# A hybrid decoder layer: another order for squares, roots, products and gates in the Z stage

## The chip, the core and the metric

The kernel runs on one core of one Trainium2 chip. Its five engines each work through an instruction queue of their own, in order: TensorE (PE, matmuls), VectorE (DVE), ScalarE (ACT), GpSimd (POOL) and SyncE (SP, which issues most DMAs). An instruction waits on semaphores that instructions of other engines, or DMAs, raise. The metric is the device time of one execution in microseconds; for one core this is the time of that core.

## The reference

One layer with two groups of heads on 1024 tokens of 1024 features, in float32. Cut to its frame:

```python
h = rms_norm(x, norm1_w[l])
proj = h @ w_in[l]
da_q, da_k, da_v, dn_qkv, dn_z, dn_a, dn_b = jnp.split(
    proj, [SPLIT_1, SPLIT_2, SPLIT_3, SPLIT_4, SPLIT_5, SPLIT_6], axis=-1)
...
dn_o = rms_norm(dn_o, dn_out_norm_w[l]) * jax.nn.silu(dn_z.reshape(B, S, DN_HEADS, DN_V_DIM))
...
x = x + mix @ w_out[l]
h = rms_norm(x, norm2_w[l])
x = x + jnp.square(jax.nn.relu(h @ w_up[l])) @ w_down[l]
```

The change is in the part that makes, for every token, the normed input `h`, the gate `silu(dn_z)` (512 columns, multiplied with `dn_out_norm_w`) and the 8 columns `dn_a`, `dn_b`. The rest (differential attention, the gated delta rule, output projection, MLP) is not touched.

## The kernel before

**Stages.** The Z stage comes first: it norms x, keeps the result for all later stages and makes the gate. Then follow the dn projections with the chunk matrices of the delta rule, the scan interleaved with attention, the output projection, and the MLP. Float32 products are made of three matmuls in the type fp32r: each operand is split into a rounded high part (`hH`, `wH`) and the rest (`hL`, `wL`), and high x high, high x low and low x high are added (L311 to L313).

**Row blocks.** The 1024 tokens are 8 blocks of 128 (`tb` 0 to 7). A block of x is loaded twice: transposed (`xTs[tb]`, features on partitions) and as rows (`xts[tb]`). The norm of a block takes these steps:

- `z_square` (L358): ACT squares the rows and adds them up per token (L361).
- `z_root` (L364): DVE forms mean plus epsilon (`nrt`, L223), POOL raises it to the power -1/2 (`nr`, L224).
- `z_diag` (L369): ACT scales an identity matrix with the roots (`dg`, L372).
- `z_spread` (L374): PE multiplies a matrix of ones with that diagonal (`ps_r`, L377). Every partition then holds the roots of the 128 tokens. It is issued inside a product, ahead of the product's step k = `at` (2 where nothing else is given).
- `z_scale` (L380 to L396): DVE multiplies the 8 feature blocks of `xT` with norm weight and roots (L388; L385 for blocks 0 and 1, which are weighed beforehand), ACT rounds two halves into `hH` (L389), DVE subtracts two halves into `hL` (L392).

**Products.** The 520 columns of gate, a and b are two units of 260 (`u` 0, 1). For blocks 0 and 1 the products run on the unscaled x (`z_raw`, L316, plain float32), and their roots are multiplied in afterwards; for blocks 2 to 7 `z_mm` (L303) makes 24 matmuls of 260 columns on `hH` and `hL`. Blocks 0 and 1 are scaled too, as later stages need them. The results lie in PSUM banks of three pools with two banks each: `pj`, `ph` and `pt_`. A fourth pool, `pm`, holds the spreads. In the kernel before, blocks 0 and 1 use `pj` (unit 0) and `ph` (unit 1), block 2 uses `pt_`, and blocks 3 to 7 only `pj`.

**Gates.** `z_gate` (L325) reads a product: a tanh on ACT (`zth`, L330), then on DVE (tanh + 1) times the product (`zg`, L331). For blocks 0 and 1 (`raw`) a second DVE instruction multiplies with root and norm weight (L334), and L338 takes the 8 columns of a and b; for the others POOL multiplies with the weight (L336) and L340 takes the 8 columns. SP stores the gate (L341). A bank comes free with its last reader: L331 for unit 0, L338 or L340 for unit 1. The gate's weight `dnw4` is halved and copied on POOL (L452, L453).

**Order.** In the Z stage the order on PE, DVE, ACT and POOL is the order in which the code is written (`tc.manual_schedule`); an instruction that waits holds up all that stand behind it on its engine. Ahead of the changed part, blocks 2 and 3 are scaled and the raw products made. In the loop over blocks 3 to 7, block tb's two products are written, then block tb+2 is scaled (its spread is in the second product), then block tb+3 is squared, rooted and made a diagonal, with the two gates of block tb among them.

**What comes behind.** `load_unit` (L183) loads 256-column units of the dn weights in four parts (`wraw`, two buffers), rounds each on ACT (L192) and subtracts on DVE (L193). The first unit takes the weight tiles of z unit 0, so its rounding can begin only when z(7,0) is done. From a and b of all blocks follow beta (L539 to L541) and the decays (L547 to L567); from those come the matrices `rrh` and `rrl` (L666) and products on PE (L668). POOL clears some tiles there (L587, L726). `trn` (L198 to L200) makes the dn products. Outside the Z stage a scheduler orders the instructions; apart from a few places next to the stage its order is the same in both kernels.

Of the kernel before, what the change touches and what calls it, by code (L numbers as in the profile page):

```python
# [22 lines left out]
NT = SEQ // P  # L23
# [97 lines left out]
def tile_hymba_layer(  # L121
# [99 lines left out]
    def rstd(o, ss, scale, eps, pool, tag, n):  # L221
        t = pool.tile([P, n], F32, tag=tag, name=tag) if pool else laid(tag)
        V.tensor_scalar(t, ss, scale, eps, ALU.mult, ALU.add)  # L223
        G.tensor_tensor(o, t, neghalf[:, :n], ALU.pow)  # L224
# [15 lines left out]
    pj = pctx.enter_context(tc.tile_pool(name="pj", bufs=2, space=PSUM))  # L240
    p1ctx = ctx.enter_context(ExitStack())
    ph = p1ctx.enter_context(tc.tile_pool(name="ph", bufs=2, space=PSUM, side="right"))
    pm = p1ctx.enter_context(tc.tile_pool(name="pm", bufs=2, space=PSUM, side="right"))
    pt_ = p1ctx.enter_context(tc.tile_pool(name="pt_", bufs=2, space=PSUM, side="right"))
# [58 lines left out]
    def z_mm(tb, u, pool=pj, tag="pj", mid=None, at=2):  # L303

        ps = pool.tile([P, 512], F32, tag=tag, name="ps_z")
        sl = slice(tb * P, (tb + 1) * P)
        wh, wl = wz[u][0]
        for k in range(KB):
            if k == at and mid is not None:
                z_spread(mid)  # L310
            T.matmul(ps[:, :UC], hH[:, k, sl], wh[:, k, :], start=k == 0, stop=False)  # L311
            T.matmul(ps[:, :UC], hH[:, k, sl], wl[:, k, :], start=False, stop=False)
            T.matmul(ps[:, :UC], hL[:, k, sl], wh[:, k, :], start=False, stop=k == KB - 1)  # L313
        return ps

    def z_raw(tb, u, pool, tag, mid=None, at=2):  # L316

        ps = pool.tile([P, 512], F32, tag=tag, name="ps_z")
        for k in range(KB):
            if k == at and mid is not None:  # L320
                z_spread(mid)
            T.matmul(ps[:, :UC], xTs[tb][:, k, :], wz[u][1][k // 2][:, k % 2, :], start=k == 0, stop=k == KB - 1)
        return ps

    def z_gate(tb, u, ps, raw=False):  # L325
        n = UC if u == 0 else 252
        th = n1.tile([P, UC], F32, tag="zth", name="zth", bufs=2)
        zg = n1.tile([P, UC], F32, tag="zg", name="zg", bufs=7)
        r = roots[tb]
        S.activation(th[:, :n], ps[:, :n], AF.Tanh, scale=half_r[tb] if raw else 0.5)  # L330
        last = V.scalar_tensor_tensor(zg[:, :n], th[:, :n], 1.0, ps[:, :n], ALU.add, ALU.mult)  # L331
        w = dnw4[:, UC * u:UC * u + n]
        if raw:
            last = V.scalar_tensor_tensor(zg[:, :n], zg[:, :n], r, w, ALU.mult, ALU.mult)  # L334
        else:
            G.tensor_tensor(zg[:, :n], zg[:, :n], w, ALU.mult)  # L336
        if u == 1 and raw:
            last = V.tensor_scalar(ab[:, tb, :], ps[:, 252:260], r, None, ALU.mult)  # L338
        elif u == 1:
            last = V.tensor_copy(ab[:, tb, :], ps[:, 252:260])  # L340
        nc.sync.dma_start(zg_d[tb, :, UC * u:UC * u + n], zg[:, :n])  # L341
        return last

    def z_round(u, i):
        S.copy(wz[u][0][0][:, 2 * i:2 * i + 2], wz[u][1][i])

    def z_rest(u, i):
        wh, wl = [x[:, 2 * i:2 * i + 2] for x in wz[u][0]]
        V.tensor_tensor(wl, wz[u][1][i], wh.bitcast(F32), ALU.subtract)
# [3 lines left out]
    def z_weigh(tb):  # L353
        for c in cuts:
            V.tensor_tensor(xTs[tb][:, c, :], xTs[tb][:, c, :], w1c[:, c].unsqueeze(2).broadcast_to([P, 4, P]),
                            ALU.mult)

    def z_square(tb):  # L358
        sq = n1.tile([P, DM], F32, tag="sq", name="sq", bufs=1)
        ss = n1.tile([P, 1], F32, tag="nss", name="nss", bufs=4)  # L360
        S.activation(sq, xts[tb], AF.Square, accum_out=ss)  # L361
        sums[tb] = ss

    def z_root(tb):  # L364

        r = roots[tb] = n1.tile([P, 1], F32, name=f"nr{tb}")
        rstd(r, sums[tb], 1.0 / DM, EPS, n1, "nrt", 1)

    def z_diag(tb):  # L369

        diags[tb] = n1.tile([P, P], F32, tag="dg", name="dg", bufs=4)
        S.activation(diags[tb], ident, AF.Copy, scale=roots[tb])  # L372

    def z_spread(tb):  # L374

        ps = pm.tile([P, 512], F32, tag="pm", name="ps_r")
        marks[tb] = T.matmul(ps[:, :P], ones, diags[tb], start=True, stop=True)  # L377
        spreads[tb] = ps[:, :P]

    def z_scale_parts(tb):  # L380
        sl = slice(tb * P, (tb + 1) * P)
        xT, last = xTs[tb], []
        for c in cuts:
            if tb < 2:
                V.tensor_tensor(xT[:, c, :], xT[:, c, :], spreads[tb].unsqueeze(1).broadcast_to([P, 4, P]), ALU.mult)  # L385
            else:
                for k in range(c.start, c.stop):
                    V.scalar_tensor_tensor(xT[:, k, :], xT[:, k, :], w1c[:, k:k + 1], spreads[tb], ALU.mult, ALU.mult)  # L388
            last.append(S.copy(hH[:, c, sl], xT[:, c, :]))  # L389
        yield  # L390
        for c in cuts:
            last.append(V.tensor_tensor(hL[:, c, sl], xT[:, c, :], hH[:, c, sl].bitcast(F32), ALU.subtract))  # L392
        yield last

    def z_scale(tb):
        return list(z_scale_parts(tb))[1]  # L396
# [17 lines left out]
    marks = {}  # L414
    with tc.manual_schedule(engines={T.engine, V.engine, S.engine, G.engine}):

        pw = pm.tile([P, 512], F32, tag="pm", name="ps_w")
        for i in range(10):
            T.transpose(pw[:, 0:P], ident, ident)
        z_weigh(0)  # L420
        z = {(0, 0): z_raw(0, 0, pj, "pj")}
        for i in range(3):
            z_round(0, i)
            z_rest(0, i)
        z_weigh(1)
        z_round(0, 3)
        z_rest(0, 3)
        z[1, 0] = z_raw(1, 0, pj, "pj")
        for i in range(4):
            z_round(1, i)  # L430
            z_rest(1, i)
        z_square(2)
        z_root(2)
        z_diag(2)
        z[0, 1] = z_raw(0, 1, ph, "ph", 2, 6)
        z_square(3)
        z_root(3)
        z_diag(3)
        z[1, 1] = z_raw(1, 1, ph, "ph", 3, 4)
        z_scale(2)  # L440
        z_square(0)
        z_square(1)
        parts = z_scale_parts(3)
        next(parts)
        for tb in range(2):
            z_root(tb)
        next(parts)
        for tb in range(2):
            half_r[tb] = n1.tile([P, 1], F32, name=f"hr{tb}")
            V.tensor_scalar(half_r[tb], roots[tb], 0.5, None, ALU.mult)  # L450
        z_square(4)
        G.tensor_scalar(dnw4[:, 0], dnw4[:, 0], 0.5, None, ALU.mult)  # L452
        G.tensor_copy(dnw4[:, 1:4], dnw4[:, 0:1].broadcast_to([P, 3, P]))  # L453
        dnw4 = dnw4.rearrange("p h e -> p (h e)")
        z[2, 0] = z_mm(2, 0, pt_, "pt")
        z_gate(0, 0, z[0, 0], True)
        z_root(4)
        z_diag(4)
        z_gate(1, 0, z[1, 0], True)
        z_gate(0, 1, z[0, 1], True)  # L460
        z[2, 1] = z_mm(2, 1, pt_, "pt", 4, 6)
        z_scale(4)
        z_square(5)
        z_gate(2, 0, z[2, 0])
        z_root(5)
        z_diag(5)
        z_gate(1, 1, z[1, 1], True)
        z_gate(2, 1, z[2, 1])
        for tb in range(3, NT):
            late = tb - 4 if 4 <= tb < 6 else None  # L470
            z[tb, 0] = z_mm(tb, 0, mid=late)
            if late is not None:
                z_scale(late)
            z[tb, 1] = z_mm(tb, 1, mid=tb + 2 if tb + 2 < NT else None)
            z_gate(tb, 0, z[tb, 0])
            if tb + 2 < NT:
                last = z_scale(tb + 2)
                if tb == 3:
                    mark = [marks[5], *last]
            if tb + 3 < NT:  # L480
                z_square(tb + 3)
                z_root(tb + 3)
                z_diag(tb + 3)
            if 3 <= tb < 5:
                z_diag(tb - 3)
            z_gate(tb, 1, z[tb, 1])


    behind = ExitStack()
# [56 lines left out]
    u, au, e, w1, lw, d1, z1 = (n32(n) for n in ("gu", "gau", "gte", "gw1", "glw", "gd1", "gz1"))  # L546
# [272 lines left out]
    pools, T_ops = {}, []  # L819
# [127 lines left out]
    late, accs = [], {}  # L947
# [393 lines left out]
    normed_by, normed_at, held_back, banks, normed2, raws, kept, u, ups = [], {}, [], {}, set(), [], {}, {}, {}  # L1341
# [410 lines left out]
    last = u_raw(4)  # L1752
# [76 lines left out]
```

## Time and profile before

| | us |
|---|---|
| median of 3 runs | 1265.45 |
| lowest, highest | 1264.93, 1265.61 |
| the profiled execution | 1262.67 |
| its span (first to last instruction) | 1261.0 |
| its mean granted PE clock | 0.996 of full speed |

A row of the view in order of time has the start in us, the duration in us, engine, line, operation, the tile written and the tiles read with their shapes, the count, and in brackets the engine's idle time before it with what ended it. A row of a stage has its limits and length, then for PE, PEld (weight load), DVE, ACT and POOL the busy us with the number of instructions, then the mean granted PE clock, the share of the DMA engines that is busy, and GB/s. The chain of waits is followed back from the last instruction to whatever released each step.

### The profile page before, as it was taken

Reading aid. Unit: us, or ns where it says so; the run is one execution under the profiler, and the core shown is the slowest. Engines: PE = TensorE matmul, PEld = TensorE weight load, DVE = VectorE, ACT = ScalarE, POOL = GpSimd, SP = SyncE. Lnnn points to the kernel's source line nnn. Section 1 sums busy time; section 2 is a strip of 40 time slices with the busy share of each in tenths; the row PEclk is TensorE's granted clock in tenths of the full one; section 3 lists DMA queues with packets and bytes.
Section 4 is the critical chain, followed back from the end, with each engine's and each line's share of the span. In section 5 each row is a group of like instructions: output and inputs, shape, how many; then the busy total and the mean of one; then the engine's idle time right before and its main releaser. Section 6 shows DMA issues by size and latency. Waiting matters only on the chain.

```text
span 1261.0 us, 18863 instructions
## 1 busy us (share of the span) xinstructions
PE 1229.8 (98%) x6887; PEld 1058.9 (84%) x6887; DVE 826.1 (66%) x1466; ACT 617.4 (49%) x1243; POOL 107.7 (9%) x139
## 2 busy tenths in 40 slices
PE   8799999999999999999999999999999999999998
PEld 7688888899998897888888888888888888888887
DVE  5757798657647647767599656655569855677553
ACT  5459654334336545666567445544555333333331
POOL 1221110012213210001210000000000000000000
PEclk9899999999999999999999999999999999999999
DMA  9134554356858656423254545343469655422311
GB/s 338 65 93 123 131 169 124 91 180 213 269 156 236 190 170 170 116 73 95 87 184 152 205 161 184 134 167 127 174 234 341 259 200 200 167 100 100 130 38 67
DMA packets 157637, 202.11 MB, mean 160 GB/s; under 512 B 20921, under 2 KB 110825, under 8 KB 157545
## 3 DMA queue, kind: packets, MB, share of 16 engines
q1 hardware_dynamic: 157400, 200.91, 49.1%
q8 instruction: 54, 0.88, 0.3%
q14 instruction: 39, 0.31, 0.1%
q10 hardware_dynamic: 144, 0.00, 0.0%
HBM read 135.86 MB, written 65.01 MB: 159 GB/s over the span
## 4 chain that ended last, share of the span: by engine, by line
PE 89%; DMA 4%; DVE 3%; ACT 2%; issue 1%; SPq 1%; POOL 0%; DVEq 0%; ACTq 0%; POOLq 0%
PE X L1428 5%; PE X L1429 5%; PE X L1430 5%; PE X L1728 4%; PE X L1727 4%; PE X L1726 4%; PE ps_dn L198 3%; PE ps_dn L200 3%; PE ps_dn L199 3%; PE ps_qk L992 3%; PE ps_qk L994 3%; PE ps_qk L993 3%; PE Y L1428 2%; PE Y L1429 2%; PE Y L1430 2%; PE ps_op L1257 2%
## 5 line engine op out<-in xcount | busy, mean ns | idle before, releaser
L1346 ACT CAST hH<-ur 128x1024 fp32r<-128x1024 f32 x56 | 58.8, 1051 | 173.3 <-PE Y L1727 90.1
L1347 DVE TENSOR_TENSOR hL<-ur,hH 128x1024 fp32r<-128x1024 f32 x56 | 68.4, 1223 | 80.3 <-ACT hH L1346 80.3
L992 PE MATMUL ps_qk<-wH,hH 128*128 128x256 f32 x384 | 114.9, 299 | 0.1
L994 PE MATMUL ps_qk<-wH,hL 128*128 128x256 f32 x384 | 108.5, 282 | 0.0
L993 PE MATMUL ps_qk<-wL,hH 128*128 128x256 f32 x384 | 108.4, 282 | 0.0
L1347 DVE TENSOR_TENSOR op<-raw,op 128x1024 fp32r<-128x1024 f32 x48 | 58.7, 1223 | 73.8 <-PE X L1429 40.8
L1726 PE MATMUL X<-hH 128*128 128x512 f32 x224 | 87.1, 389 | 0.0
L1727 PE MATMUL X<-hL,hH 128*128 128x512 f32 x224 | 87.1, 389 | 0.0
L1728 PE MATMUL X<-hH,hL 128*128 128x512 f32 x224 | 87.1, 389 | 0.0
L198 PE MATMUL ps_dn<-hH,wH 128*128 128x512 f32 x192 | 76.2, 397 | 0.2 <-ACT cp L611 0.2
L200 PE MATMUL ps_dn<-hH,wL 128*128 128x512 f32 x192 | 76.0, 396 | 0.0
L199 PE MATMUL ps_dn<-hL,wH 128*128 128x512 f32 x192 | 75.8, 395 | 0.0
L992 PEld LDWEIGHTS ps_qk<-wH,hH 128*128 128x128 f32 x384 | 73.5, 191 | 0.3 <-ACT qn L1011 0.2
L993 PEld LDWEIGHTS ps_qk<-wL,hH 128*128 128x128 f32 x384 | 73.5, 191 | 0.0
L994 PEld LDWEIGHTS ps_qk<-wH,hL 128*128 128x128 f32 x384 | 73.2, 191 | 0.0
L1347 DVE TENSOR_TENSOR hL<-dw,hH 128x1024 fp32r<-128x1024 f32 x56 | 68.1, 1218 | 0.9 <-ACT hH L1346 0.9
L1346 ACT CAST op<-raw 128x1024 fp32r<-128x1024 f32 x48 | 50.4, 1051 | 36.0 <-PE Y L1430 19.9
L193 DVE TENSOR_TENSOR wL<-wraw,wH 128x512 fp32r<-128x512 f32 x64 | 43.7, 696 | 34.8 <-ACT wH L192 34.5
L1346 ACT CAST hH<-dw 128x1024 fp32r<-128x1024 f32 x56 | 58.7, 1049 | 10.7 <-DMA dw<-in_w_down_dram 5.0
L192 ACT CAST wH<-wraw 128x512 fp32r<-128x512 f32 x64 | 38.2, 620 | 45.2 <-DMA wraw<-in_w_units_dram 31.7
L615 DVE SCALAR_TENSOR_TENSOR cy<-cp,pv,cy 128x512 f32<-128x512 f32 x72 | 53.7, 747 | 8.1 <-ACT cy L613 7.3
L1121 ACT ACTIVATE pexp<-ps_sc,mx 128x128 f32<-128x128 f32 (+7 forms) x64 | 47.3, 740 | 20.0 <-DVE mx L1117 19.9
(362 smaller groups left out, 3442.0 us busy)
## 6 DMA issues: line engine op xcount, KB each, us to landing
ur<-ud SPq DMA_DIRECT2D x28, 1024.0 KB, 5.1
raw<-in_w_up_dram SPq DMA_DIRECT2D x32, 512.0 KB, 4.0
dw<-in_w_down_dram SPq DMA_DIRECT2D x32, 512.0 KB, 6.5
wraw<-in_w_units_dram SPq DMA_DIRECT2D x48, 256.0 KB, 3.7
qk_d<-qa SPq DMA_DIRECT2D x32, 256.0 KB, 3.4
ud<-ua SPq DMA_DIRECT2D x16, 512.0 KB, 4.1
ud<-s SPq DMA_DIRECT2D x16, 512.0 KB, 2.6
pka<-park_d SPq DMA_DIRECT2D x32, 192.0 KB, 4.2
```

The lines of the kernel that those rows point to most:

```text
L198: T.matmul(ps, lh(k), rh(k), start=(k == 0), stop=False)
L199: T.matmul(ps, lh(k), rl(k), start=False, stop=False)
L200: T.matmul(ps, ll(k), rh(k), start=False, stop=(k == n - 1))
L992: T.matmul(ps[:, :256], hH[:, k, sl], wh[:, k, :], start=(k == 0), stop=False)
L993: T.matmul(ps[:, :256], hH[:, k, sl], wl[:, k, :], start=False, stop=False)
L994: T.matmul(ps[:, :256], hL[:, k, sl], wh[:, k, :], start=False, stop=(k == KB - 1))
L1346: S.copy(dst[0], src)
L1347: V.tensor_tensor(dst[1], src, dst[0].bitcast(F32), ALU.subtract)
L1428: T.matmul(ps, op[0][:, k, cs], h[0][:, k, :], start=start and k == 0, stop=False, skip_group_check=True)
L1726: T.matmul(bank[t], v[0][:, j, sl], v[2][:, j], start=s0, stop=False, skip_group_check=True)
L1727: T.matmul(bank[t], v[0][:, j, sl], v[3][:, j], start=False, stop=False, skip_group_check=True)
L1728: T.matmul(bank[t], v[1][:, j, sl], v[2][:, j], start=False, stop=s1, skip_group_check=True)
```

## The change

Only the manual order of the Z stage changes, and the banks that its products use:

- Root and diagonal of block 4 come right behind its square, ahead of the first gate; block 5 is squared between the first two gates, block 6 ahead of z(3,0), block 7 ahead of z(3,1).
- Blocks 3 to 7 use the pools `pj`, `ph`, `pt_`, `pj`, `ph` in turn, six banks instead of two.
- The spreads move: block 4's into z(3,0) at step 1, 5's into z(3,1) at step 3, 6's into z(4,1) at 1, 7's into z(5,0) at 3, 0's into z(5,1) at 3, 1's into z(6,0) at 3. The scaling of each follows the product that holds its spread.
- The gates are written by a list behind these scalings: those of (0,1) and (1,1) behind z(3,0), of block 2 behind z(3,1), of block 3 behind z(4,1), of block 4 behind z(5,0), and so on; the last two behind z(7,1).
- The diagonals of blocks 0 and 1 both come behind that of block 7.

In the order that results outside the Z stage three things differ: the transposition to `ps_pv`, which uses a bank of `ph`, stands in the first dn product instead of between z(3,1) and z(4,0); DVE has L540 and L541 ahead of the L193 of the third weight part instead of behind it; and on SP the stores of the gates stand elsewhere among the small loads. Lines behind the changed part are two higher in the kernel after.

```diff
         z_square(4)
+        z_root(4)
+        z_diag(4)
         G.tensor_scalar(dnw4[:, 0], dnw4[:, 0], 0.5, None, ALU.mult)
         G.tensor_copy(dnw4[:, 1:4], dnw4[:, 0:1].broadcast_to([P, 3, P]))
         dnw4 = dnw4.rearrange("p h e -> p (h e)")
+
+        pools = {3: (pj, "pj"), 4: (ph, "ph"), 5: (pt_, "pt"), 6: (pj, "pj"), 7: (ph, "ph")}
         z[2, 0] = z_mm(2, 0, pt_, "pt")
         z_gate(0, 0, z[0, 0], True)
-        z_root(4)
-        z_diag(4)
+        z_square(5)
+        z[2, 1] = z_mm(2, 1, pt_, "pt")
         z_gate(1, 0, z[1, 0], True)
-        z_gate(0, 1, z[0, 1], True)
-        z[2, 1] = z_mm(2, 1, pt_, "pt", 4, 6)
-        z_scale(4)
-        z_square(5)
-        z_gate(2, 0, z[2, 0])
+        roots_due = {(3, 0): (6,), (3, 1): (7,)}
+        gates_due = {(3, 0): ((0, 1), (1, 1)), (3, 1): ((2, 0), (2, 1)), (4, 1): ((3, 0), (3, 1)),
+                     (5, 0): ((4, 0), (4, 1)), (5, 1): ((5, 0),), (6, 0): ((5, 1),), (6, 1): ((6, 0),),
+                     (7, 0): ((6, 1),), (7, 1): ((7, 0), (7, 1))}
+        spread_at = {(3, 0): (4, 1), (3, 1): (5, 3), (4, 1): (6, 1), (5, 0): (7, 3), (5, 1): (0, 3), (6, 0): (1, 3)}
         z_root(5)
         z_diag(5)
-        z_gate(1, 1, z[1, 1], True)
-        z_gate(2, 1, z[2, 1])
         for tb in range(3, NT):
-            late = tb - 4 if 4 <= tb < 6 else None
-            z[tb, 0] = z_mm(tb, 0, mid=late)
-            if late is not None:
-                z_scale(late)
-            z[tb, 1] = z_mm(tb, 1, mid=tb + 2 if tb + 2 < NT else None)
-            z_gate(tb, 0, z[tb, 0])
-            if tb + 2 < NT:
-                last = z_scale(tb + 2)
-                if tb == 3:
-                    mark = [marks[5], *last]
-            if tb + 3 < NT:
-                z_square(tb + 3)
-                z_root(tb + 3)
-                z_diag(tb + 3)
-            if 3 <= tb < 5:
-                z_diag(tb - 3)
-            z_gate(tb, 1, z[tb, 1])
+            for u in range(2):
+                for b in roots_due.get((tb, u), ()):
+                    z_square(b)
+                nxt, at = spread_at.get((tb, u), (None, 0))
+                z[tb, u] = z_mm(tb, u, *pools[tb], nxt, at)
+                if nxt is not None:
+                    last = z_scale(nxt)
+                    if nxt == 5:
+                        mark = [marks[5], *last]
+                for b in roots_due.get((tb, u), ()):
+                    z_root(b)
+                    z_diag(b)
+                if (tb, u) == (3, 1):
+                    z_diag(0)
+                    z_diag(1)
+                for b, v in gates_due.get((tb, u), ()):
+                    z_gate(b, v, z[b, v], b < 2)
```

## The prediction

> **What bounds the kernel now.** First the page: span, busy shares, chain.
>
> ```profile
> span 1261.0 us, 18863 instructions
> ...
> PE 1229.8 (98%) x6887; PEld 1058.9 (84%) x6887; DVE 826.1 (66%) x1466; ACT 617.4 (49%) x1243; POOL 107.7 (9%) x139
> ...
> PE 89%; DMA 4%; DVE 3%; ACT 2%; issue 1%; SPq 1%; POOL 0%; DVEq 0%; ACTq 0%; POOLq 0%
> ```
>
> TensorE (PE) is 98% busy, so only a stage with PE gaps can give anything. Next the busy time by stage: the Z products that the change reorders (21.4 to 74.8), the start of the dn projections, what follows.
>
> ```profile
> 21.40:74.80 53.40, 42.05 (x303) 40.97 (x302) 34.71 (x105) 23.30 (x51) 13.29 (x19) 0.90 0.32 113
> 74.80:89.00 14.20, 12.77 (x61) 10.11 (x59) 8.54 (x28) 8.24 (x20) 3.59 (x7) 1.00 0.50 130
> 89.00:200.00 111.00, 111.00 (x597) 93.29 (x598) 92.03 (x237) 77.53 (x255) 16.14 (x15) 1.00 0.52 142
> ```
>
> In the Z stage PE is idle for 11.4 us and its clock averages 0.90; after 89 us it is busy without a gap for over 100 us. So an earlier Z end moves everything behind it by as much. Third, PE in order of time:
>
> ```profile
> 24.50 0.28 PE L311 MATMUL ps_z<-wH,hH 128*128 128x260 f32 x1
> ...
> 26.52 0.28 PE L313 MATMUL ps_z<-wH,hL 128*128 128x260 f32 x1
> 28.98 0.76 PE L377 MATMUL ps_r<-dg,ones 128*128 128x128 f32 x2 [2.17 <-ACT dg L372]
> ...
> 30.19 0.42 PE L311 MATMUL ps_z<-wH,hH 128*128 128x260 f32 x1
> ...
> 32.14 0.42 PE L311 MATMUL ps_z<-wH,hH 128*128 128x260 f32 x1
> ...
> 37.63 0.49 PE L377 MATMUL ps_r<-dg,ones 128*128 128x128 f32 x2 [2.31 <-ACT dg L372]
> ...
> 45.54 0.49 PE L377 MATMUL ps_r<-dg,ones 128*128 128x128 f32 x2 [4.17 <-ACT dg L372]
> ...
> 56.23 0.70 PE L377 MATMUL ps_r<-dg,ones 128*128 128x128 f32 x2 [2.70 <-ACT dg L372]
> ...
> 74.80 0.40 PE L198 MATMUL ps_dn<-hH,wH 128*128 128x512 f32 x1
> ```
>
> Four stalls, 11.35 us, all at a spread (L377) that waits for its diagonal (L372), the end of square, root, diagonal. The 0.28 us rows are 17 steps apart, 0.119 us each; the 0.42 us rows 9 steps, 0.217 us: after the gaps of 2.17, 4.17 and 2.70 the first 15 or so matmuls run at half speed (1.5 us lost each), after that of 2.31 they do not. A product is 24 steps, 2.87 us.
>
> **The change part by part.** No arithmetic is added: 12 products, 6 spreads, the same gates. What changes is the order on each engine, so I walk it, writing z(b,u) for block b, unit u. Prices come from rows where the consumer was waiting (ACT, then DVE, then POOL):
>
> ```profile
> 14.24 1.06 ACT L361 ACTIVATE sq<-xt 128x1024 f32<-128x1024 f32 x1 [1.93 <-DMA xt<-in_x_dram]
> ...
> 16.25 0.40 ACT L372 ACTIVATE dg<-ident,nr 128x128 f32<-128x128 f32 x1 [0.86 <-POOL nr L224]
> ...
> 25.19 1.06 ACT L361 ACTIVATE sq<-xt 128x1024 f32<-128x1024 f32 x1 [0.70 <-DMA xt<-in_x_dram]
> ...
> 32.31 0.62 ACT L389 CAST hH<-xT 128x512 fp32r<-128x512 f32 x1 [2.66 <-DVE xT L388]
> 33.35 0.63 ACT L389 CAST hH<-xT 128x512 fp32r<-128x512 f32 x1 [0.41 <-DVE xT L388]
> ...
> 37.17 0.40 ACT L372 ACTIVATE dg<-ident,nr 128x128 f32<-128x128 f32 x1 [1.88 <-POOL nr L224]
> 37.48 0.45 ACT L330 ACTIVATE zth<-ps_z,hr 128x252 f32<-128x252 f32 x1
> ```
>
> ```profile
> 15.43 0.15 DVE L223 TENSOR_SCALAR nrt<-nss 128x1 f32<-128x1 f32 x1 [2.06 <-ACT sq L361]
> ...
> 31.16 2.15 DVE L388 SCALAR_TENSOR_TENSOR xT<-xT,w1c,ps_r 128x128 f32<-128x128 f32 x8
> 33.23 1.47 DVE L392 TENSOR_TENSOR hL<-xT,hH 128x512 fp32r<-128x512 f32 x2
> ...
> 37.96 0.42 DVE L331 SCALAR_TENSOR_TENSOR zg<-zth,ps_z 128x252 f32<-128x252 f32 x1 [2.15 <-ACT zth L330]
> 38.41 0.48 DVE L334 SCALAR_TENSOR_TENSOR zg<-zg,nr,dnw 128x252 f32<-128x252 f32 x1
> 38.81 0.22 DVE L338 TENSOR_SCALAR ab<-ps_z,nr 128x8 f32<-128x8 f32 x1
> 38.95 0.41 DVE L331 SCALAR_TENSOR_TENSOR zg<-zth,ps_z 128x252 f32<-128x252 f32 x1
> ```
>
> ```profile
> 15.66 0.55 POOL L224 TENSOR_TENSOR nr<-nrt,neghalf 128x1 f32<-128x1 f32 x1 [13.17 <-DVE nrt L223]
> ...
> 25.69 0.62 POOL L452 TENSOR_SCALAR dnw<-dnw 128x128 f32<-128x128 f32 x1
> 26.38 0.50 POOL L453 COPY dnw<-dnw 128x384 f32<-128x384 f32 x1
> ```
>
> Root chain: square to nrt 1.19, nrt to nr 0.23, nr to diagonal 0.59; 0.31 later ACT issues the next. Raw gate: tanh to L331 0.48, to L334 0.45, to L338 0.40, next gate 0.14 on. Scaling: casts 1.15 and 2.19 after the first L388, the low part done at 3.54.
>
> *Block 4.* Its square stays at 25.19, but root and diagonal now come before the gate of z(0,0): diagonal at 25.19+1.19+0.23+0.59=27.20, and the first stall is gone. That gate's tanh, which came right behind the square, moves behind the diagonal to 27.51. z(3,0) reuses its bank and now waits for L331 to end, 28.42, while PE has finished z(2,1) at 24.50+2.87=27.37: a new stall of 1.1. The weights of the gate (L452, L453) stand behind nr4 on POOL: 25.19+1.19+0.23=26.61, +0.55+1.19=28.35, in time for L334 at 28.45.
>
> *Blocks 5 and 6.* Square 5 at 27.88, tanh of z(1,0) 28.94, L331 29.43, L334 29.88, and only then nrt5 at 30.29: diagonal 31.11, in time for its spread at 32.8. The scaling of block 4 starts at 30.37. Square 6 takes ACT from 31.42 to 32.48, so the cast due at 31.52 waits 1.0; second low part from 33.73, nrt6 34.34, diagonal 6 at 35.16. Square 6 needs its row block, which is issued here and lands at 29.7 by the DMA row; were it 1 us later, all below is 0.4 late.
>
> ```profile
> 22.22 1.41 SPq L277 DMA_DIRECT2D xt<-in_x_dram  x2
> ...
> DMA to landing us min/median/max: 7.5/7.5/7.5
> ```
>
> *The third bank pair.* z(4,0) takes the bank of z(0,1), whose gate stands behind diagonal 6 on ACT: tanh 35.47, L331 35.96, L334 36.41, L338 36.81, bank free 37.05. PE is through with z(3,1) at 28.45+0.2 (the first matmul after a wait)+2x(2.87+0.24)=34.9, a spread being two matmuls or 0.24. Second new stall, 2.2. Behind that diagonal also wait tanh(1,1), square 7 and the casts of block 5.
>
> *Block 7.* Gate of z(1,1) on DVE at 36.95; scaling of block 5 at 37.94, second cast 40.13, second low part 40.79, nrt7 41.40, diagonal 7 at 42.22. Two more diagonals (0 and 1), then the tanh of z(2,0) at 43.15, its L331 from 43.57 to 43.99: z(5,0) may start at 44.0. PE has done z(4,0) and z(4,1) at 43.3, or 44.7 if they start at half speed. I take half speed (two of three gaps between 2.17 and 2.70 had it): z(5,0) at 44.7.
>
> *From there PE is the bound*: DVE's 34.7 us of work in this stage fit into 21.4 to 62 with 6 to spare. Six products of 2.87 and three spreads of 0.24 are 17.9. No other wait comes last there: z(6,0), at 51.0, needs a low part that ends at 47.8 (scaling of block 6 from 44.3, 3.5 long), z(7,0), at 57, one that ends at 52 (from 48.5). Z ends at 62.6, warm at 62.0. Before: 74.8. Gain 12.2 (warm 12.8).
>
> *Stores and loads.* The first two gate stores go later on SP, behind the lambda loads; the two weight loads queued after them are wanted when z(7,0) frees the weight tiles, at 59 now.
>
> ```profile
> 34.76 0.43 SPq L191 DMA_DIRECT2D wraw<-in_w_units_dram  x1
> ```
>
> With an issue at about 35 they have some 24 us of cover. The transposition to ps_pv moves out of Z to the dn stage: 0.2 less there, 0.2 more here, nothing.
>
> *The tail.* Here I expect a loss:
>
> ```profile
> 77.67 0.69 DVE L193 TENSOR_TENSOR wL<-wraw,wH 128x512 fp32r<-128x512 f32 x1 [0.69 <-ACT wH L192]
> 78.28 1.32 DVE L540 TENSOR_SCALAR beta<-beta 128x32 f32<-128x32 f32 x1
> ```
>
> ```profile
> 77.53 1.93 POOL L726 MEMSET gb<- 128x512 f32 x4
> ```
>
> ```profile
> 80.66 3.06 DMA wraw<-in_w_units_dram
> ```
>
> ```profile
> 85.43 1.28 ACT L666 ACTIVATE rrh<-tri,gghr 128x128 fp32r<-128x128 f32 x4 [1.07 <-DVE gghr L566]
> ```
>
> These are DVE, POOL, the chain of waits and ACT. L540, on 32 columns, lasts until the memsets end at 79.5; L193, sixteen times its size, ran through them in 0.69. In the changed order L540 comes ahead of the L193 of the third weight part, whose raw tile must be free before a later part is loaded. Counted from the Z end: L540 is due at 2.2 and held until 4.8, its reciprocal takes 0.3, so the third part's L193 moves from 2.9 to 5.1 and the fourth's ends at 6.6, where before it ended at 80.66-74.80=5.9. From there the load, the cast, L193 and the gate chain to rrh take 4.8 as before (80.66 to 85.43), and PE's next product but one waits for rrh: 0.8 late (6.6-5.9=0.7, and some rounding). Bounds: -0.4 (not held, and the loads before it leave earlier) and +1.0. I take 0.8, since L540 is due inside the memsets.
>
> [...]
>
> Sum: 12.2-0.8=11.4. The profiled execution took 1262.67 (span 1261.0 and 1.67 around it), so 1251.3 for such an execution; the median of the runs, 1265.45, is 2.78 higher, and I carry the gain over as it is: **1254.1**.
>
> **The rivals.**
> 1. *No half speed after the 2.2 gap*: 12.8-0.8=12.0, 1253.4. For it: the gap of 2.31. Against: those of 2.17 and 2.70. [...]
> 2. *More stalls of that kind*, one of 2.2 each at z(5,0) and z(6,0), because my chain is too short: 11.4-4.4=7.0, 1258.4. For it: every chain crosses three engines, and I summed starts without slack for any of them. Against: blocks 6 and 7 have 3 us of room and more.
> 3. *The chain is shorter than I sum*, down to where PE runs on from 28.5: ten products and six spreads end at 28.5+28.7+1.4=58.6, gain 16.2-0.8=15.4, 1250.0. For it: the gates of z(0,1) and z(1,1) could be done early if ACT reached them early. Against: they stand behind diagonal 6, and that behind square 6 and the casts of block 4.
> 4. *Slower*: a bank on any of the six is freed only by a gate, and gates now stand behind roots and scalings. If that costs each product 2.2 and a start at half speed (1.5), 3.7 in all, the kernel loses from the fourth such product on (14.8 against 11.4); with five, 1272.6. For it: exactly this happens at z(4,0). Against: from z(5,0) on the gates stand behind scalings that are ahead of PE by 3 us.
> 5. *No effect*: the dn stage takes the time back, waiting for weights that land no sooner: 1265. For it: the chain of waits there runs through their loads. Against: these wait for freed tiles, not for a time, and the DMA engines are half busy (0.50).
>
> **How the numbers follow.** Forecast 0.46, rival 1 0.27, rival 2 0.13, rival 3 0.06, rival 4 0.04, rival 5 0.04. A measurement tells 0.2% (2.5 us) from no change. Faster: 0.46+0.27+0.13+0.06=0.92; same 0.04; slower 0.04. Range 1249.8 to 1258.6: from rival 3 to rival 2, which takes in the bounds of the tail (-0.4 and +1.0) and of the late row block (0.4); it leaves out rivals 4 and 5.
>
> **What would show it.** dn's first matmul at 62 to 63 us; no wait over 0.3 us at L377; PE gaps before L311 of about 1.1 at 28.5, 2.2 at 37.1, none over 1 after 45; L540 before the third L193, and rrh at 73 to 75. Wrong if a gap over 1.5 us stands behind 46, or if dn starts after 67.

## The result, and the profile after

| | before | after |
|---|---|---|
| median of the runs, us | 1265.45 | 1251.69 |
| lowest, highest (5 runs each) | 1263.56, 1265.84 | 1249.38, 1256.73 |
| ratio of the times, 95% interval | | 0.990, 0.9877 to 0.9923 |
| the profiled execution | 1262.67 | 1251.69 |
| its span | 1261.0 | 1250.0 |
| its mean granted PE clock | 0.996 | 0.997 |

The changed kernel is 1.0% faster, 13.8 us by the medians and 11.0 by the two profiled executions. In the views of the kernel after, L540 is L542 and L666 is L668.

First the page after: span, busy shares, chain of waits.

```profile
span 1250.0 us, 18861 instructions
...
PE 1226.3 (98%) x6887; PEld 1055.9 (84%) x6887; DVE 824.5 (66%) x1466; ACT 616.7 (49%) x1243; POOL 107.4 (9%) x139
...
PE 90%; DMA 5%; DVE 2%; ACT 2%; issue 1%; SPq 0%; POOL 0%; DVEq 0%; ACTq 0%
```

DVE, ACT and POOL are as busy as they were (within 1.6 us). PE is idle for 7.5 us less and busy for 3.5 us less. The same stages as before, cut where they now end (busy us and count of PE, PEld, DVE, ACT, POOL, then the mean granted PE clock):

```profile
21.40:62.77 41.37, 38.18 (x304) 37.74 (x302) 33.04 (x103) 22.57 (x51) 11.66 (x18) 0.96 0.40 141
62.77:76.96 14.19, 13.23 (x62) 10.20 (x61) 9.06 (x31) 8.40 (x20) 4.85 (x9) 1.00 0.50 148
76.96:188.00 111.04, 111.04 (x597) 93.33 (x598) 91.27 (x236) 77.38 (x255) 16.14 (x15) 1.00 0.51 141
```

The Z stage took 53.40 us and takes 41.37. PE idles in it for 3.2 us instead of 11.4, which is 8.2 of the 12.0 us; the other 3.9 are busy time (38.18 instead of 42.05). The same matmuls take less of it because one stretch of 3.41 us in Z has a granted clock of 0.5, where before there were three (mean clock 0.96 instead of 0.90). Such a stretch is called a half-speed spell below. The two stages behind it are as long as they were (14.20 and 111.00). All of the gain is made in Z, and none is given back in the 125 us behind it. PE in order of time:

```profile
28.67 0.39 PE L311 MATMUL ps_z<-wH,hH 128*128 128x260 f32 x1 [1.02 <-DVE zg L331]
...
29.13 0.39 PE L377 MATMUL ps_r<-dg,ones 128*128 128x128 f32 x2
...
32.95 0.38 PE L377 MATMUL ps_r<-dg,ones 128*128 128x128 f32 x2
...
37.30 0.36 PE L311 MATMUL ps_z<-wH,hH 128*128 128x260 f32 x1 [2.16 <-DVE ab L338]
...
42.14 0.38 PE L377 MATMUL ps_r<-dg,ones 128*128 128x128 f32 x2
...
62.77 0.40 PE L198 MATMUL ps_dn<-hH,wH 128*128 128x512 f32 x1
```

Not one spread (L377) waits any more. Two new waits stand at L311, both for a bank that a gate has not yet read, and behind it, between 37.30 and 62.77 there is none. What those gates stood behind is seen on ACT and DVE:

```profile
27.39 0.40 ACT L372 ACTIVATE dg<-ident,nr 128x128 f32<-128x128 f32 x1 [0.85 <-POOL nr L224]
...
35.30 0.40 ACT L372 ACTIVATE dg<-ident,nr 128x128 f32<-128x128 f32 x1 [1.53 <-POOL nr L224]
35.61 0.81 ACT L330 ACTIVATE zth<-ps_z,hr 128x252 f32<-128x252 f32 x2
```

```profile
36.94 0.22 DVE L338 TENSOR_SCALAR ab<-ps_z,nr 128x8 f32<-128x8 f32 x1
```

The tanh of z(0,1) needs nothing but PE's result of long ago, yet it starts at 35.61, right behind the diagonal of block 6; its L338 ends at 37.16 and PE starts at 37.30.

The tail, on DVE, POOL and ACT:

```profile
64.86 1.67 DVE L542 TENSOR_SCALAR beta<-beta 128x32 f32<-128x32 f32 x1
66.56 0.35 DVE L543 RECIPROCAL beta<-beta 128x32 f32<-128x32 f32 x1
66.83 0.63 DVE L193 TENSOR_TENSOR wL<-wraw,wH 128x512 fp32r<-128x512 f32 x1
```

```profile
64.60 0.96 POOL L589 MEMSET fg<- 128x1024 f32 x1
65.49 1.00 POOL L728 MEMSET gb<- 128x512 f32 x2
67.08 1.02 POOL L728 MEMSET gb<- 128x512 f32 x2 [0.59 <-POOL gb L728]
```

```profile
73.35 1.28 ACT L668 ACTIVATE rrh<-tri,gghr 128x128 fp32r<-128x128 f32 x4 [1.07 <-DVE gghr L568]
```

L542 is held until 66.53, to the end of the first two gb memsets; then the third L193 runs, and rrh comes 73.35-62.77=10.58 after the Z end. Before it was 85.43-74.80=10.63.

### The profile page after: what moved, and what is told of

It is laid out like the page before. It is cut to its first block, busy times and chain, and to the rows that moved or that the text cites. A ratio compares the mean times of both kernels' runs of the same rounds, so it can differ in the third digit from the quotient of the medians.

```text
span 1250.0 us, 18861 instructions
## 1 busy us (share of the span) xinstructions
PE 1226.3 (98%) x6887; PEld 1055.9 (84%) x6887; DVE 824.5 (66%) x1466; ACT 616.7 (49%) x1243; POOL 107.4 (9%) x139
## 4 chain that ended last, share of the span: by engine, by line
PE 90%; DMA 5%; DVE 2%; ACT 2%; issue 1%; SPq 0%; POOL 0%; DVEq 0%; ACTq 0%
PE X L1432 5%; PE X L1430 5%; PE X L1431 5%; PE X L1729 4%; PE X L1728 4%; PE X L1730 4%; PE ps_dn L198 3%; PE ps_dn L200 3%; PE ps_dn L199 3%; PE ps_qk L994 3%; PE ps_qk L995 3%; PE ps_qk L996 3%; PE Y L1432 2%; PE Y L1430 2%; PE Y L1431 2%; PE ps_op L1259 2%
## 5 line engine op out<-in xcount | busy, mean ns | idle before, releaser
L199 PE MATMUL ps_dn<-hL,wH 128*128 128x512 f32 x192 | 75.8, 395 | 0.0
L193 DVE TENSOR_TENSOR wL<-wraw,wH 128x512 fp32r<-128x512 f32 x64 | 43.0, 686 | 38.3 <-ACT wH L192 38.2
L1348 ACT CAST hH<-dw 128x1024 fp32r<-128x1024 f32 x56 | 58.7, 1048 | 10.7 <-DMA dw<-in_w_down_dram 4.9
```

The costliest lines, as they stand in the source:

```text
L199: T.matmul(ps, lh(k), rl(k), start=False, stop=False)
L1348: S.copy(dst[0], src)
```

## The experiments

Each was compared with runs of the kernel before on its own chip. "Changed kernel" is the kernel after, and "dn" stands for the first matmul of the dn products, where the Z stage ends.

**The banks alone.** The kernel before, in its old order, with six banks:

```diff
+        pools = {3: (pj, "pj"), 4: (ph, "ph"), 5: (pt_, "pt"), 6: (pj, "pj"), 7: (ph, "ph")}
         for tb in range(3, NT):
...
-            z[tb, 0] = z_mm(tb, 0, mid=late)
+            z[tb, 0] = z_mm(tb, 0, *pools[tb], late)
...
-            z[tb, 1] = z_mm(tb, 1, mid=tb + 2 if tb + 2 < NT else None)
+            z[tb, 1] = z_mm(tb, 1, *pools[tb], tb + 2 if tb + 2 < NT else None)
```

> Only the bank rotation of the change: the kernel before with blocks 3 to 7 on six banks in turn, in its old order. Theory (order, not banks, was the limit before, as all four stalls of PE stood at L377 behind a diagonal): the four stalls stay, 11.4 us within 0.5, and the first dn matmul starts at 74.8 within 0.3; ratio to the kernel before 0.999 to 1.001. Rival (banks alone give part of the gain, since a product could start before its gate): the first dn matmul comes at least 2 us earlier, ratio 0.998 or below.

Measured: 1265.07 against 1265.10, ratio 0.9997 (0.9984 to 1.001). The view of PE's waits (us in total, times, longest):

```profile
PE ps_r L377 <- ACT dg L372: 10.1, 4, 3.1
```

The four stalls stay, and the banks alone are worth nothing. Two numbers of the profiled execution fell outside both theories: the stalls come to 10.1 us, not 11.4, and dn starts at 73.0, not 74.8. The runs don't show these 1.8 us. They arise between the third stall and the fourth. The spread that ends the third stall comes at 45.39, 0.15 ahead of the kernel before (45.54), the one that ends the fourth at 54.53, 1.70 ahead (56.23). In between the kernel before runs a spell at half speed and this execution none; the one that it has behind the second stall instead falls into the third, which is 3.06 long here and 4.17 there. So the difference goes with the granted clock; why a spell comes or not is treated in the last section.

**The order with four banks.** The changed kernel with the banks of `pj` and `pt_` for blocks 3 to 7, none of `ph`:

```diff
-        pools = {3: (pj, "pj"), 4: (ph, "ph"), 5: (pt_, "pt"), 6: (pj, "pj"), 7: (ph, "ph")}
+        pools = {3: (pj, "pj"), 4: (pt_, "pt"), 5: (pj, "pj"), 6: (pt_, "pt"), 7: (pj, "pj")}
```

> The changed kernel with its new order, but only the four banks of the first and third pool for blocks 3 to 7 (block 3 the first, 4 the third, and so on). Theory (the new order puts gates behind roots and scalings, so it needs the six banks): z(4,0) now waits for the L331 of z(2,0), which stands behind the diagonals of blocks 7, 0 and 1, until some 44 us; a gap of about 9 us at L311, a start at half speed, and a further wait of about 2 at z(5,0); the first dn matmul at 70 to 73, some 9 us behind the changed kernel, ratio to the kernel before 0.996 to 1.000. Rival (banks do not matter in this order either): first dn matmul at 62.8 within 0.5, ratio 0.988 to 0.992.

Measured: 1262.08, ratio 0.9975 (0.9965 to 0.9986); dn starts at 72.4. PE:

```profile
37.31 0.24 PE L508 MATMUL ps_pv<-ident,rows 50*128 50x50 f32 x1 [2.15 <-issue]
44.16 0.58 PE L311 MATMUL ps_z<-wH,hH 128*128 128x260 f32 x1 [6.62 <-DVE zg L331]
...
54.38 0.39 PE L311 MATMUL ps_z<-wH,hH 128*128 128x260 f32 x1 [1.45 <-DVE zg L331]
```

As the theory had it: 2.15 and 6.62 us of gap ahead of z(4,0), with only the small transposition between them, a start at half speed (0.58 us for the first matmul), and 1.45 at z(5,0). With the first run this shows that neither half does it without the other: six banks in the old order give 0.0 us, the new order with four banks 3.0, both together 13. The new order with the two banks of before was not run. The order moves gates behind roots and scalings, and only the third pair of banks lets PE run on meanwhile. It also shows rival 4's mechanism at work, at z(4,0) and smaller at z(5,0).

**The first new stall.** The first tanh ahead of the diagonal of block 4:

```diff
         z_root(4)
-        z_diag(4)
...
         z_gate(0, 0, z[0, 0], True)
+        z_diag(4)
         z_square(5)
```

> The changed kernel with the diagonal of block 4 behind the first gate, so that the tanh of z(0,0) comes about 0.4 to 0.7 us earlier on ACT. Theory (the first new stall only shifts into the second, as z(4,0) waits for L338 of z(0,1) however early PE gets there): the gap of 1.0 at z(3,0) falls to 0.5 or less, the one at z(4,0) grows by the same amount to about 3, the first dn matmul stays at 62.8 within 0.4. Rival (each stall costs by itself): first dn matmul 0.6 to 1.0 earlier, at about 61.8 to 62.2, and the gap at z(4,0) stays at 2.2.

Measured: 1252.48, ratio 0.9902 (0.9887 to 0.9917). The stall at z(3,0) is gone and the other has grown from 2.16 to:

```profile
36.84 0.36 PE L311 MATMUL ps_z<-wH,hH 128*128 128x260 f32 x1 [3.26 <-DVE ab L338]
```

dn starts at 62.3, 0.5 earlier, just beyond the 0.4 allowed; ACT's square of block 4 ended 0.5 earlier in this execution too (its row block landed earlier), so that much need not be the edit's; the changed kernel itself, unaltered, had dn at 62.29 in a later profile. The stall moved, as the theory said: the first was covered by the second.

**The second new stall.** The gates of z(0,1) and z(1,1) directly behind the diagonal of block 5:

```diff
         z[2, 1] = z_mm(2, 1, pt_, "pt")
+        z_root(5)
         z_gate(1, 0, z[1, 0], True)
+        z_diag(5)
+        z_gate(0, 1, z[0, 1], True)
+        z_gate(1, 1, z[1, 1], True)
...
-        gates_due = {(3, 0): ((0, 1), (1, 1)), (3, 1): ((2, 0), (2, 1)), (4, 1): ((3, 0), (3, 1)),
+        gates_due = {(3, 1): ((2, 0), (2, 1)), (4, 1): ((3, 0), (3, 1)),
...
-        z_root(5)
-        z_diag(5)
```

> The changed kernel with the gates of z(0,1) and z(1,1) right behind the diagonal of block 5, and the root of block 5 ahead of the gate of z(1,0) on DVE: the bank of z(4,0) then comes free at about 33.5 instead of 37. Theory (the second stall is set by where this gate stands, behind the diagonal of block 6): the gap of 2.2 before z(4,0) falls to 0.4 to 0.8, now ended by the low part of block 4; no half-speed start in the Z stage; first dn matmul at 60.0 to 60.8, some 2.4 earlier than in the changed kernel, ratio to the kernel before 0.986 to 0.990 (by its median of 1251.7, some 1249.3). Rival (the scaling of block 4 and what follows is pushed back by the two gates on DVE by as much, so that PE waits at z(4,0) or z(5,0) instead): first dn matmul at 62.3 or later, a gap of over 1.5 us at another product.

Measured: 1249.26, ratio 0.9881 (0.9865 to 0.9898); dn at 60.84. PE, then DVE:

```profile
35.44 0.39 PE L313 MATMUL ps_z<-wH,hL 128*128 128x260 f32 x1 [0.28 <-DVE hL L392]
42.82 0.39 PE L311 MATMUL ps_z<-wH,hH 128*128 128x260 f32 x1 [1.39 <-DVE zg L331]
```

```profile
31.52 0.22 DVE L338 TENSOR_SCALAR ab<-ps_z,nr 128x8 f32<-128x8 f32 x1
```

L338 of the same gate is at 31.52 instead of 36.94, and the gap of 2.16 has become 0.28, now ended by the low part of block 4. So it was the gate's place that set it, not anything that the gate needs. The half-speed spell is gone as well. Of the 2.4 us expected 1.9 came, which is just outside the stated 60.0 to 60.8, and a new wait of 1.39 stands at z(5,0), a smaller form of the rival.

**That wait too.** On top of the last: the root and diagonal of block 6 ahead of the scaling of block 4, those of block 7 and the gates of block 2 ahead of the scaling of block 5, the first tanh ahead of diagonal 4:

```diff
...
                 z[tb, u] = z_mm(tb, u, *pools[tb], nxt, at)
+                if (tb, u) == (3, 0):
+                    z_root(6)
+                    z_diag(6)
+                if (tb, u) == (3, 1):
+                    z_gate(2, 0, z[2, 0])
+                    z_gate(2, 1, z[2, 1])
                 if nxt is not None:
...
```

> Gates of z(0,1) and z(1,1) early as in the run before, and besides: root and diagonal of block 6 ahead of the scaling of block 4, root and diagonal of block 7 and the gates of block 2 ahead of the scaling of block 5, the first tanh ahead of diagonal 4. Theory (the two stalls that were left, 0.8 at z(3,0) and 1.4 at z(5,0), stand behind ACT's place for two tanh and nothing else): all waits at L311 together under 1.0, first dn matmul at 59.0 to 59.9, that is 1 to 1.8 ahead of the run before, ratio to the kernel before 0.984 to 0.988. Rival (the scalings, written later now, become the wait: PE stands at L313 or L311 for a low or high part of block 4 or 5): one such wait over 1.0, first dn matmul at 60.5 or later, ratio as before, 0.988.

Measured: 1249.83, ratio 0.9877 (0.9857 to 0.9896); dn at 59.90. No wait at L311 is left, and one of 0.34 at L313. The times can't tell 0.9 us from nothing, as the interval is 5 us wide, but the trace shows that it was lost behind dn. DVE, and ACT, in the tail:

```profile
61.97 1.89 DVE L550 TENSOR_SCALAR beta<-beta 128x32 f32<-128x32 f32 x1
```

```profile
70.99 1.28 ACT L676 ACTIVATE rrh<-tri,gghr 128x128 fp32r<-128x128 f32 x4 [1.07 <-DVE gghr L576]
```

The beta addition is held for 1.89 us, and rrh comes 11.1 after the Z end; in the run before it came at 70.49, 9.7 after it. PE feels it: from dn to its 54th matmul at L199, some 50 us behind, it takes 51.06 us, in the run before 49.62. So this matmul comes 0.5 later than there. What Z won, the tail took.

**The tail's hold.** The changed kernel, with POOL's memsets behind the decays:

```diff
     V.tensor_tensor(gglr, gg, ggh, ALU.subtract)
+    late = G.tensor_copy(sp.tile([P, 1], F32, name="gate1"), gg[:, 0:1])
...
-    G.memset(fg, 0.0)
-    G.memset(fg[:, ::33], 1.0)
+    with tc.issue_after(late.ins):
+        G.memset(fg, 0.0)
+        G.memset(fg[:, ::33], 1.0)
...
-        G.memset(gb, 0.0)
+        with tc.issue_after(late.ins):
+            G.memset(gb, 0.0)
```

> The changed kernel, with POOL's clearing of the two kinds of tiles behind the decays (one tiny POOL copy of a decay column ahead of it makes it wait). Theory (POOL's memsets hold the 32-column beta instruction, which holds the third weight part's L193): the beta addition takes 0.3 or less instead of 1.67, the third L193 starts 2.5 to 3.0 after the Z end instead of 4.1, the fourth ends some 1.0 earlier, rrh starts 9.4 to 9.9 after the Z end instead of 10.6; time 0.3 to 0.8 below the changed kernel's, as PE waits only 0.7 for rrl there. Rival (the addition waits for its input, and the memsets beside it mean nothing): it takes 1.6 again or starts 1.5 later, rrh at 10.6 after the Z end, same time as the changed kernel within 0.3.

Measured: 1249.51, ratio 0.9878 (0.986 to 0.9897), dn at 62.01. DVE and ACT:

```profile
64.10 0.18 DVE L542 TENSOR_SCALAR beta<-beta 128x32 f32<-128x32 f32 x1
64.31 0.35 DVE L543 RECIPROCAL beta<-beta 128x32 f32<-128x32 f32 x1
64.58 0.63 DVE L193 TENSOR_TENSOR wL<-wraw,wH 128x512 fp32r<-128x512 f32 x1
```

```profile
71.45 1.28 ACT L670 ACTIVATE rrh<-tri,gghr 128x128 fp32r<-128x128 f32 x4 [1.07 <-DVE gghr L568]
```

The same instruction takes 0.18 instead of 1.67; the third L193 starts 2.57 after the Z end (4.06 in the changed kernel), rrh comes 9.44 after it (10.58). The memsets did hold it. To its 54th matmul at L199 PE takes 49.38 us from dn, in the changed kernel 50.56, so the trace gains 1.2 us, more than the 0.3 to 0.8 expected.

Not every DVE instruction was held by memsets: in the kernel before, L193, with two inputs, ran beside them in 0.69 us, as without them (0.63 and 0.69 in the run with late memsets). Beside POOL's product L336, which reads two tiles where a memset reads none, two L193 took 1.85 together in the kernel before; two took 1.30 in the run with late memsets, with L336 all but over. L336 itself took 1.24 instead of 0.75:

```profile
73.06 1.85 DVE L193 TENSOR_TENSOR wL<-wraw,wH 128x512 fp32r<-128x512 f32 x2
```

```profile
73.12 1.24 POOL L336 TENSOR_TENSOR zg<-zg,dnw 128x260 f32<-128x260 f32 x1 [2.16 <-DVE zg L331]
```

That the beta addition, which has one input, is held by memsets is shown (1.67 beside them, 0.18 without them); why it is held and L193 is not, no run shows.

**Both.** The early gates and roots together with the late memsets:

> The gates and roots as in the first run of this call together with the late memsets. Theory: the two gains add, first dn matmul as in that run, rrh 9.4 to 9.9 after it, time 0.3 to 0.8 below that run's. Rival (with PE ahead by more, the tail is bound by the weight loads instead): rrh at more than 10.2 after the Z end, time as that run's.

Measured: 1248.10, ratio 0.9862 (0.984 to 0.9884). PE:

```profile
59.23 0.40 PE L198 MATMUL ps_dn<-hH,wH 128*128 128x512 f32 x1
```

rrh comes at 68.8, 9.6 after it. The two gains add in the trace: PE's 54th matmul at L199 comes 4.6 earlier than in the changed kernel, with the early gates and roots alone 2.4, with the late memsets alone 1.9. The time is 1.7 us below that of the early gates and roots, more than the 0.3 to 0.8 expected, though the two intervals overlap. This is the lowest median of all.

**The changed kernel again**, on the chip of the last three:

> The changed kernel itself, unaltered, on the same chip as the three others, for a comparison of times. Expected 1251.7 within 1.0, and in the profile a half-speed spell in the Z stage or none, as the 2.2 gap falls against the clock's grid of 3.4 us: if at least 1.8 of it lie in one cell of the grid, a half-speed spell follows, otherwise none (theory); rival: after every gap of 2.1 or more.

Measured: 1251.57, ratio 0.9899 (0.9882 to 0.9917). Of its gap before z(4,0), 2.19 us here, 2.17 lie in one cell of the clock's grid (cells of 3.41 us, see the last section), and a half-speed spell follows. In the kernel with late memsets the same gap, 2.17, falls 1.68 into one cell and 0.49 into the next, and none follows: the theory, not the rival.

**Once more, three of them on another chip**, since the intervals overlapped.

> The changed kernel with the late memsets once more, since its interval overlapped the changed kernel's. Theory (the hold costs PE the 0.7 us wait for rrl and little more): 0.3 to 1.0 below the changed kernel of this call. Rival (2 us, as the first medians had it, 1249.5 against 1251.6): 1.5 or more below. Clock rule: wherever PE is idle 1.95 us or more of a 3.41 us cell of the clock's grid the next cell is at half speed, at 1.75 or less at full.

> Early gates and roots with late memsets once more. Theory (3.5 us earlier at the first dn matmul, 4.5 at rrh, of which some is given back in the stages behind): 2.5 to 4.5 below the changed kernel of this call, no half-speed cell in the Z stage. Rival (what is won here is lost again before the end): within 1.5 of it.

> The changed kernel unaltered, for the comparison with the two others of this call: 1251.6 within 1.0. Clock rule as for the first run of this call; the gap of 2.2 before z(4,0) comes again, and a half-speed cell follows if 1.95 or more of it lie in one cell (theory), or always (rival).

Measured (us):

| | on this chip | ratio, interval | on the chip before |
|---|---|---|---|
| changed kernel | 1252.21 | 0.9905, 0.9885 to 0.9925 | 1251.57 |
| memsets late | 1250.52 | 0.9894, 0.9876 to 0.9912 | 1249.51 |
| both | 1248.41 | 0.9873, 0.9853 to 0.9894 | 1248.10 |

The version with both edits is 3.5 and 3.8 below the changed kernel, within what was expected, and its rrh comes 9.9 after the Z end here. The pairs of intervals overlap by 0.0002 and 0.0009, but the order is the same on both chips. The memsets alone are 2.1 and 1.7 below the changed kernel, where 0.3 to 1.0 was expected; by these medians the rival, 1.5 or more, came nearer. But the intervals overlap by about half. The traces are firmer: from dn to the 54th matmul at L199 PE takes 49.38 and 49.36 us with late memsets, 50.56 and 50.70 in the changed kernel on the first two occasions (in the third a half-speed spell lies in between). That is 1.2 to 1.3 us; whether the time gains more than that stays open. In the changed kernel's profile on this chip the gap of 2.17 lay 1.12 and 1.05 in two cells, and again no half-speed spell followed in the Z stage.

## Why the prediction was right

1. *Roots ahead.* Diagonal 4 was forecast for 27.20 and came at 27.39, since the row block landed 0.2 later than before; all four stalls at L377 are gone. The other diagonals too came 0.1 to 0.2 after their forecast (35.30 for 35.16).
2. *The two new stalls.* Forecast 1.1 at z(3,0) and 2.2 at z(4,0), with the instructions that end them, L331 and L338; measured 1.02 and 2.16, ended by these. The fourth run showed that the place of the gate sets the second, the third that it covers the first.
3. *Half speed after it.* Taken, and so it was in the profiled execution; but that was luck. The reason given, two of three earlier gaps, doesn't decide it: of the three profiles of the changed kernel two have the spell and one doesn't, by where the gap falls (last section), so rival 1 is what happens in some executions. The size was about right. In this order of the Z stage dn starts at 62.77 and 62.56 with the spell, and at 62.01, 62.20 and 62.29 without it: 0.5 on average, where the two forecasts of the Z end, 62.6 and 62.0, are 0.6 apart. Without the spell PE waits 0.7 for the bank of z(5,0), as the walk of ACT's order had it.
4. *PE the bound from there.* Z end forecast 62.6, came at 62.77, with no wait behind 37.3. Gain at dn's start forecast 12.2, measured 74.80-62.77=12.03.
5. *The tail: the one term of the sum that was mis-sized*, 0.8 against 0.0. The mechanism was right (held 1.67; freed of it, rrh is 1.1 to 1.3 earlier). But I had L542 held until all four gb memsets were over; POOL paused for 0.59 us after two and L542 ended there, so the third L193 came at 4.06 after the Z end, not 5.1. And the fourth part, which I let follow the third, had its cast earlier, not later: at 3.28 after the Z end where before it was at 4.48, waiting for its load in both. So its L193 ended at 5.67 and not at 6.6. Before had lost as much there by that wait, and I compared with it as if it had none. ACT before, then after:

```profile
79.28 0.62 ACT L192 CAST wH<-wraw 128x512 fp32r<-128x512 f32 x1 [1.36 <-DMA wraw<-in_w_units_dram]
```

```profile
66.05 0.62 ACT L192 CAST wH<-wraw 128x512 fp32r<-128x512 f32 x1 [0.85 <-DMA wraw<-in_w_units_dram]
```

6. *From the span to the median.* The span fell by 11.0, where 11.4 was forecast. That the two are so close is partly luck: the 0.8 of the tail were not lost, and 1.0 that the sum does not have was lost later. Matched matmul by matmul, PE's lead on the kernel before is 12.0 at 113 us, 13.0 at 320, 11.9 at 396, 10.7 at 408 and 11.0 at the end; it wanders with the waits behind 300 us, and falls by 1.2 across a half-speed spell at 400 us. By the medians the gain is 13.8, so that 1251.69 stands against a forecast of 1254.1. The interval of the ratio allows 9.7 to 15.6, and the same comparison on two other chips gave 13.0 and 11.7, so these 2.4 are not clear of noise. A part of them may be the step "I carry the gain over as it is": before's profiled execution was 2.8 faster than its median, after's was its median (last section).
7. *The rivals.* Rival 4's mechanism exists (four banks), rival 3's figure of 58.6 for a chain without stalls is what both edits come near to (59.23). Rival 5 is refuted for the change, whose two stages behind Z are as long as before, but the run with early gates and roots shows its kind: 0.9 us won in Z and 1.4 lost by the 54th matmul at L199.

## What to carry to other kernels

Where one engine runs an order written by hand, look for instructions that have long had their inputs and stand behind a chain that crosses three engines: whoever needs the buffer that they free waits for the whole chain (here PE, 2.16 us at z(4,0)). More buffers and an earlier chain can each be worth little without the other (0.0 and 3.0 of 13 us here), since the one only uncovers the other's wait. And compare sums with medians only after looking at how many half-speed spells the profiled execution happened to have (before's, at a mean clock of 0.996, was 2.8 us faster than its median).

## What was not expected of the hardware

**The clock's grid.** By the traces' record of the granted clock, half-speed spells (but for one that is running when the record ends) last 3.41 us or a multiple of it (10.24 with four banks, where the mean clock from 21.4 to 62.7 is 0.88), and in one execution they all lie on one grid of 3.41 us: before, they begin at 29.05, 46.12 and 56.36, 5 and 3 cells apart, after, at 38.43 and 400.25, 106 cells apart. The place of the grid differs from execution to execution. Stages cut along that grid (length, PE's busy us, at the end the granted clock): after, the kernel with late memsets, and the one with six banks and the old order.

```profile
35.02:38.43 3.41, 1.25 (x11) 1.16 (x10) 2.27 (x8) 2.15 (x5) 0.24 (x1) 1.00 0.61 151
38.43:41.85 3.42, 3.42 (x18) 3.42 (x17) 3.34 (x13) 1.35 (x3) 0.13 (x1) 0.50 0.51 179
```

```profile
33.18:36.59 3.41, 1.73 (x15) 1.51 (x13) 1.92 (x5) 1.88 (x5) 0.55 (x1) 1.00 0.59 140
36.59:40.01 3.42, 2.93 (x24) 2.96 (x25) 3.38 (x14) 1.26 (x4) 0.00 (x0) 1.00 0.56 195
```

```profile
27.00:30.41 3.41, 1.46 (x12) 1.46 (x13) 1.77 (x6) 1.13 (x3) 0.58 (x2) 1.00 0.93 321
30.41:33.82 3.41, 3.41 (x18) 3.41 (x18) 3.37 (x12) 1.12 (x2) 0.00 (x0) 0.50 0.24 76
...
40.65:44.06 3.41, 1.68 (x14) 1.47 (x13) 3.32 (x14) 2.38 (x5) 0.18 (x1) 1.00 0.23 79
44.06:47.48 3.42, 2.09 (x17) 2.09 (x18) 2.19 (x8) 1.89 (x6) 1.28 (x2) 1.00 0.00 0
```

With 1.25 or 1.46 us busy in a cell the next is at half speed, with 1.68 or 1.73 it is not. Of the cells of the Z stage at full speed that were cut so in six profiles (before, after, six banks in the old order, late memsets, and the changed kernel twice more), those with 1.95 us idle or more were followed by half speed, those with 1.75 or less were not. The smallest of these gaps to be followed by half speed was one of 1.98, with 1.95 in one cell (six banks in the old order). The last pair of rows is a gap of 3.06, the longest of its profile, that lies across two cells and goes free. The gap of 2.31 in the kernel before, which went free and which the prediction left without a reason, lies across two cells as well, with 1.75 in the second. In the stages behind Z the bound does not hold: in the third profile of the changed kernel a cell with 1.13 idle (73.85 to 77.26) was followed by half speed, in the kernel before one with 1.46 (411.34 to 414.75) was not. So the rule as it was put down ahead of the last three runs fails outside Z.

So the gap of 2.2 was followed by half speed in some executions of the changed order (after, and the changed kernel again: 2.16 and 2.19) and not in others (late memsets, and the third time: 2.17 each), and a good part of the spread of the times goes with the granted clock. The six runs of the kernel with late memsets on the last chip, mean granted clock and time:

```
1.000 1248.39
0.998 1249.53
0.997 1250.40, 1250.63, 1250.83
0.996 1251.91
```

On the same chip the kernel before had four runs at a clock of 0.996 or 0.997, of 1261.54 to 1262.65 us, and seven at 0.991 to 0.993, of 1263.75 to 1267.46. Its profile, taken on another occasion at 0.996, looks like the lighter kind. The tie is looser elsewhere: with both edits one run took 1250.78 at 0.999 and another 1246.57 at 0.998, and on the first experiments' chip the kernel before took from 1263.67 to 1267.62 at 0.993. So the clock is not all of the spread. By my estimate a kernel with four gaps in Z (three spells there in its profile) has more chances of such spells than one with a single gap of that size (one spell or none), which would make the change worth more in the median than in the pair of profiles; no profile of a slower run shows where its spells lie, so this is not shown.

The same chance took part of the gain at 400 us. Two cells of before, where the gap is split, and two of after:

```profile
407.93:411.34 3.41, 2.02 (x17) 1.81 (x16) 1.44 (x4) 0.70 (x2) 0.53 (x1) 1.00 0.93 307
411.34:414.75 3.41, 1.95 (x17) 1.96 (x18) 1.92 (x5) 2.79 (x8) 0.00 (x0) 1.00 0.68 213
```

```profile
396.84:400.25 3.41, 1.25 (x11) 1.04 (x9) 0.40 (x2) 0.15 (x1) 0.00 (x0) 1.00 0.89 279
400.25:403.66 3.41, 2.72 (x13) 2.73 (x14) 2.69 (x6) 3.06 (x8) 0.00 (x0) 0.50 0.55 166
```

**A tiny instruction held.** An addition on 32 columns took 0.74, 1.32, 1.67 or 1.89 us where POOL's clearing lay beside it (early gates, before, after, early gates and roots), and 0.18 and 0.17 where it did not (late memsets, and both edits). Each hold ended within 0.15 us of the end of a memset, in one case of the first beside it, in the others only of a later one. The profile counts the hold as the instruction's own time (1.67 for the same 32 columns as 0.18), so here its length is the sign of it.
